# Nine products at another address distance behind each set of block products, and earlier transposes, in the first FFN of a two-layer decoder trunk

## The chip, the cores and the metric

The kernel runs on one core of a Trainium2 chip. The metric is device time in microseconds of one execution; the time before is 930.26, the median of three runs (929.63 to 930.61). TensorE multiplies (a stationary operand is loaded, a moving operand is streamed past it), VectorE and ScalarE do the element-wise work, GpSimd some of it, and the SyncE queue issues nearly all loads of weights.

## The reference, cut to what matters

Two layers over 256 tokens of width 1024. Each layer adds half an FFN, a mixer, and half an FFN again:

```python
def swiglu(x, w_gate, w_up, w_down):
    return (jax.nn.silu(x @ w_gate) * (x @ w_up)) @ w_down
...
    for layer in range(DEPTH):
        h = h + 0.5 * swiglu(rms_norm(h, ffn1_norm[layer]),
                             ffn1_w_gate[layer], ffn1_w_up[layer], ffn1_w_down[layer])
        hn = rms_norm(h, mix_norm[layer])
...
            h = h + ab_mixer(hn, ab_w_in[i], ab_v_norm[i], ab_w_spatial[i],
                             ab_b_spatial[i], ab_w_out[i])
...
        h = h + 0.5 * swiglu(rms_norm(h, ffn2_norm[layer]),
                             ffn2_w_gate[layer], ffn2_w_up[layer], ffn2_w_down[layer])
    return rms_norm(h, final_norm)
```

The FFN's inner width is 2816, which is 22 tiles of 128. All is float32. The change touches the first FFN of layer 0 and the way from it into the mixer of layer 0.

## The kernel before

**Three products for one.** A float32 product is made of three: each operand is split into a high part (ScalarE copies it to the type fp32r) and a low part (VectorE subtracts the high part). `mm3` (L384 to L387) issues high x high, high x low and low x high into one bank of PSUM. So products come in threes, with the lines L385, L386, L387.

**Weights come as chunks.** `weight_chunks` lists them in order of use; `Stream` loads each into one of three `raw` tiles, splits it into one of four pairs of tiles `whi` and `wlo`, and frees the pair when TensorE has done its chunk. The split of a chunk therefore waits until the chunk four places ahead of it is used up. A chunk of 256 columns has eight row tiles k (six in the last chunk of a down block) and gives 48 products (36).

**Two kinds of product.** In gate, up and most down products the weights are the stationary operand (128 columns of one row tile) and the activations, `xTh`/`xTl` or `hTh`/`hTl`, are streamed, 256 tokens wide. In the *block products* the roles are exchanged. The first FFN is "woven": the left 512 columns of its down product are made with seven block products (times three, 21) in place of eight for each pair of inner tiles, between the other chunks (`seven_products`, stationary `hTh`, `hTl` or their sums `hSh`, `hSl`, streamed weights). There are eleven sets of them: from the fifth gate and up pair on, one set behind each pair; the seventh follows the sixth directly, and then one behind each of the down chunks that come next. `gather_first` puts the seven results of all sets together into four quarters, which are transposed by TensorE against `ident` (`turned`, L784) and added to x.

**Address distance.** Tiles of the activations and the split tiles start on a multiple of 256 bytes in each partition. A chunk's split weights are placed `SHIFT` = 16 floats further, 64 bytes. Weights of block products are placed at 48 floats and the sums so that they start on a multiple of 256. So stationary and moving operand stand 64 bytes apart, modulo 256, in both kinds of product. A chunk with `reset` = 3 places the left 128 columns of its first three row tiles elsewhere in the tile, at 52 floats modulo 64 (208 bytes): the nine products that use them come first and have another distance. These columns and the right ones beside them are split as two strided pieces of 384 elements, the rest as one of 1280; without `reset` a chunk is split in two halves of 1024. The third chunk of this FFN and several chunks of the mixers have `reset` already.

**The way into the mixer.** `Next.pair(i, p, ...)` adds a pair of 128-row tiles of the FFN's result to x (VectorE: `part`, then `x`), makes their scaled high parts `xTh` (ScalarE) and low parts `xTl` (VectorE), and sums squares for the norm. Pairs 0 and 1 come from the transposes of the quarters, pairs 2 and 3 from the third and fourth column blocks of the down product. `first_tiles` begins the mixer: products with row tiles 0 to 5 of two column tiles, then 6 and 7, then the next chunk, where `everywhere` multiplies the split sum of squares by a matrix of ones (L478, L479); from the mean it makes `row`, which scales the queries and keys. The first scores (L1117) need a key that GpSimd finishes (L1096, L1098).

**What sets the order.** Code order, but for a scheduler that works ahead of the run: it places each engine's instructions by its own estimate of when operands are there. Each engine then works through its list in order. `issue_after` fixes some places.

Of the kernel before, what the change touches and what calls it, by code (L numbers as in the profile page):

```python
# [15 lines left out]
S = 256  # L16
# [4 lines left out]
FT = FF // 128  # L21
# [15 lines left out]
LINE, SHIFT = 64, 16  # L37
EDGE, GAP = 56, 240

RESET, RESHIFT = 3, 52  # L40
# [9 lines left out]
LAG = 4  # L50
# [5 lines left out]
def weight_chunks():  # L56

    chunks = []

    def add(m, r, n, c0, c1, shift=0, cuts=(), reset=0, summed=False, kind="N"):  # L60
        chunks.append((m[:-1], m[-1], r, n, c0, c1, shift, cuts, reset, summed, kind))

    def cols(m, c0, w, cuts=(), reset=0):
        n = CH // w
        for k in range(0, KD, n):
            add(m, k * 128, n, c0, c0 + w, SHIFT if w == 256 else 0, cuts, reset)

    def ffn(name, layer, last=False, again=(2, 3), woven=False):
        first = len(chunks)
        wd = (f"{name}_w_down", layer)  # L70

        def seven(pair):
            add(wd, pair * 256, 2, 0, 512, MSHIFT, kind="S")

        for c in range(0, FF, 256):
            if len(chunks) == 0:
                for k in (0, 4):
                    add((f"{name}_w_gate", f"{name}_w_up", layer), k * 128, 4, c, c + 256, SHIFT,
                        (1, 2, 3) if k else (0.5, 1, 1.5, 2, 3))
                continue  # L80
            for m in ("gate", "up"):
                n = len(chunks)
                cuts = (6,) if first == 0 and n in again else ()
                cols((f"{name}_w_{m}", layer), c, 256, cuts, RESET if n - first in again else 0)
            if woven and c // 256 >= LAG:
                seven(c // 256 - LAG)
        if last:
            for i in range(FT // 2):
                add(wd, i * 256, 2, 0, D, kind=LAST[i])
            return  # L90
        rest = list(range(FT // 2 - LAG, FT // 2)) if woven else []
        if woven:
            seven(rest.pop(0))
        for c in range(512 if woven else 0, D, 256):
            for k, n in DOWN:
                add(wd, k * 128, n, c, c + 256, SHIFT)
                if rest:
                    seven(rest.pop(0))

    def mix(m, order, summed=False):  # L100
        for k in order[:4:2]:
            add(m, k * 128, 2, 0, D, SHIFT)
        for c in (0, 512):
            add(m, order[4] * 128, 4, c, c + 512, SHIFT, summed=summed and c == 0)

    ffn("ffn1", 0, again=(2,), woven=0 in WOVEN)
    wab = ("ab_w_in", 0)
    cols(wab, 0, 256)
    cols(wab, 512, 256, reset=RESET)
    cols(wab, 1024, 512)  # L110
    cols(wab, 2048, 512)
    for c, n in ((1536, RESET), (1792, 0), (256, RESET), (768, RESET)):
        cols(wab, c, 256, reset=n)
    mix(("ab_w_out", 0), MIX1)
    ffn("ffn2", 0, again=(2,), woven=2 in WOVEN)
    ffn("ffn1", 1, again=(), woven=3 in WOVEN)
    wc = ("c_w_in", 0)
    for c in range(4):
        cols(wc, c * 256, 256, reset=RESET if c % 2 else 0)
        cols(wc, 1024 + c * 256, 256, reset=0 if c else RESET)  # L120
        if c % 2 == 0:
            cols(wc, 2048 + c * 256, 512)
    mix(("c_w_out", 0), MIX2, True)
    ffn("ffn2", 1, True, again=(2,))
    return chunks
# [217 lines left out]
def trunk(ctx: ExitStack, tc: tile.TileContext, a, out):  # L343
# [40 lines left out]
    def mm3(p, sh, sl, mh, ml, start, stop):  # L384
        nc.tensor.matmul(p, sh, mh, start=start, stop=False)  # L385
        nc.tensor.matmul(p, sh, ml, start=False, stop=False)  # L386
        return nc.tensor.matmul(p, sl, mh, start=False, stop=stop)  # L387
# [297 lines left out]
    def ffn(phase):  # L685
        nonlocal nxt
        with tc.tile_pool(name="fp", bufs=1) as fp:
            hT = [fp.tile([128, FT, S], F32R, name=n) for n in ("hTh", "hTl")]
            last = phase == 5
            woven = phase in WOVEN  # L690
# [99 lines left out]
            for n in range(FT):  # L790
                k, m = n - n % 2, n % 2
# [49 lines left out]
            for c in range(2 if woven else 0, 4):  # L841
                b = bank()
                for k0, n in DOWN:
                    w = st.take()
                    for kk in range(n):
                        k = k0 + kk
                        for j in range(2):
                            cs = slice(j * 128, (j + 1) * 128)
                            mm3(b[:, j * S : (j + 1) * S], w[0][kk][:, cs], w[1][kk][:, cs], hT[0][:, k], hT[1][:, k],
                                k == j == 0, k == FT - 1 and j == 1)  # L850
                    if woven and c == 3 and k0:
                        turned(k0 // 16, quarters[k0 // 16])
                    if k0 + n == FT:
                        nxt.pair(c, b, row, fp)
                    st.free()
                    if rest:
                        seven_products(rest.pop(0))
                        if not rest:
                            quarters = gather_first()
# [593 lines left out]
```

## Time and profile before

| | us |
|---|---|
| median of three runs | 930.26 |
| profiled execution | 929.4 |
| its span in the trace | 927.7 |
| TensorE busy in the span | 917.6 |
| VectorE busy | 730.0 |
| ScalarE busy | 544.9 |

The stages around the change, by their starts in TensorE's timeline: gate and up products alone to 60.80; then sets of block products between the pairs to 147.91; down products with the last sets between to 170.65; the fourth column block to 186.50, with the transposes at 181.96 and 186.50; the mixer from 186.85; its first row products (512 wide) from 200.56; the first scores at 210.01. A row of the timeline has the start, the duration, the engine, the line, the operation, what it writes and reads, and how many such instructions were merged; a matmul's duration runs to the end of its pipeline, so the pace is read from the starts. In brackets stand the idle time ahead and what ended it.

### The profile page before, as it was taken

The numbers are of one execution on the slowest core, as the hardware profiler recorded it, in microseconds if no ns is written. First come the engines' busy times: TensorE is split into PE (matmuls) and PEld (weight loads), VectorE is DVE, ScalarE is ACT, GpSimd is POOL, SyncE is SP. The second block draws the span as 40 slices with busy tenths as digits, with TensorE's granted clock in tenths as the row PEclk, the third lists the DMA queues.
The fourth block names the chain that finished last, engine by engine and source line by source line (L and its number), as shares of the span: only waits on it lengthen the run. The fifth ranks groups of instructions, "written<-read, shape, count | busy, mean of one in ns | idle before, by whom it ended". The sixth has DMA issues, their size and how long they took to land.

```text
span 927.7 us, 18344 instructions
## 1 busy us (share of the span) xinstructions
PE 917.6 (99%) x7558; PEld 898.2 (97%) x7558; DVE 730.0 (79%) x1152; ACT 544.9 (59%) x830; POOL 84.0 (9%) x117
## 2 busy tenths in 40 slices
PE   9999999999999999999999999999999999999997
PEld 9999999988999999999999999999999999999886
DVE  7999797888878856675677766757788799978896
ACT  7766455568667644444564444445776767545574
POOL 0000000016220000000000000001555200000002
PEclk9999999999999999999999999999999999999999
DMA  9646555754336587785656877855533466755691
GB/s 322 248 160 228 192 179 189 258 204 164 131 127 242 223 272 273 273 295 177 221 184 246 302 270 297 344 201 210 182 137 137 108 231 229 274 195 204 221 311 58
DMA packets 34707, 202.17 MB, mean 218 GB/s; under 512 B 3984, under 2 KB 6288, under 8 KB 13760
## 3 DMA queue, kind: packets, MB, share of 16 engines
q1 hardware_dynamic: 33120, 197.79, 59.6%
q0 software_dynamic: 496, 1.77, 0.8%
q10 hardware_dynamic: 1008, 1.44, 0.4%
q8 instruction: 59, 0.97, 0.4%
q14 instruction: 24, 0.20, 0.1%
HBM read 188.14 MB, written 12.85 MB: 217 GB/s over the span
## 4 chain that ended last, share of the span: by engine, by line
PE 91%; issue 4%; DVE 2%; DMA 1%; POOL 1%; ACT 1%; POOLq 0%; DVEq 0%
PE bank L386 29%; PE bank L385 29%; PE bank L387 29%; DVE wlo L253 1%; PE bank L633 1%; PE bank L1155 1%; DMA x<-blocks 1%; DMA xTl<-away 0%; PE bank L636 0%; PE bank L609 0%; POOL xTl L899 0%; ACT whi L246 0%; PE bank L1117 0%; PE bank L1119 0%; PE bank L1118 0%
## 5 line engine op out<-in xcount | busy, mean ns | idle before, releaser
L246 ACT ACTIVATE whi<-raw 128x1024 fp32r<-128x1024 f32 (+5 forms) x359 | 340.8, 991 | 243.1 <-PE bank L386 110.2
L253 DVE TENSOR_TENSOR wlo<-raw,whi 128x1024 fp32r<-128x1024 f32 (+5 forms) x359 | 402.2, 1148 | 56.5 <-ACT whi L246 55.3
L385 PE MATMUL bank<-xTh,whi 128*128 128x256 f32 x1600 | 443.3, 277 | 1.3 <-ACT xTh L421 1.3
L386 PE MATMUL bank<-xTl,whi 128*128 128x256 f32 x1600 | 442.4, 277 | 0.4 <-DVE xTl L424 0.4
L387 PE MATMUL bank<-xTh,wlo 128*128 128x256 f32 x1600 | 442.3, 277 | 0.0
L385 PEld LDWEIGHTS bank<-xTh,whi 128*128 128x128 f32 x1600 | 300.3, 188 | 1.6 <-ACT xTh L421 1.5
L386 PEld LDWEIGHTS bank<-xTl,whi 128*128 128x128 f32 x1600 | 300.9, 188 | 0.6 <-DVE xTl L424 0.6
L387 PEld LDWEIGHTS bank<-xTh,wlo 128*128 128x128 f32 x1600 | 300.2, 188 | 0.0
L385 PE MATMUL bank<-hTh,whi 128*128 128x256 f32 x440 | 121.9, 277 | 0.0
L387 PE MATMUL bank<-hTh,wlo 128*128 128x256 f32 x440 | 121.8, 277 | 0.0
L386 PE MATMUL bank<-hTl,whi 128*128 128x256 f32 x440 | 121.8, 277 | 0.0
L386 PEld LDWEIGHTS bank<-hTl,whi 128*128 128x128 f32 x440 | 82.9, 188 | 0.0
L385 PEld LDWEIGHTS bank<-hTh,whi 128*128 128x128 f32 x440 | 82.6, 188 | 0.0
L387 PEld LDWEIGHTS bank<-hTh,wlo 128*128 128x128 f32 x440 | 82.6, 188 | 0.0
L720 DVE TENSOR_TENSOR hm<-gs,bank 128x512 f32<-128x512 f32 x44 | 29.9, 684 | 33.4 <-PE bank L387 33.2
L1050 POOL MEMSET k<- 64x256 f32 x12 | 3.2, 306 | 572.0 <-ACT whi L246 379.2
L717 DVE TENSOR_TENSOR gs<-bank,row 128x512 f32<-128x512 f32 x44 | 30.1, 685 | 11.4 <-PE bank L387 11.3
L1146 POOL TENSOR_SCALAR pr<-pr,rl 128x128 f32<-128x128 f32 (+1 forms) x36 | 34.0, 957 | 25.8 <-DVE rl L1142 18.6
L718 ACT ACTIVATE gs<-gs 128x512 f32<-128x512 f32 x44 | 27.2, 621 | 14.7 <-DVE gs L717 14.7
L385 PE MATMUL bank<-mixh,whi 128*128 128x256 f32 x128 | 35.7, 279 | 0.0
L387 PE MATMUL bank<-mixh,wlo 128*128 128x256 f32 x128 | 35.4, 277 | 0.0
L386 PE MATMUL bank<-mixl,whi 128*128 128x256 f32 x128 | 35.4, 276 | 0.0
(247 smaller groups left out, 1152.4 us busy)
## 6 DMA issues: line engine op xcount, KB each, us to landing
raw<-in_weights SPq DMA_DIRECT2D x135, 1024.0 KB, 5.0
blocks<-in_weights SPq DMA_DIRECT2D x9, 1024.0 KB, 11.1
blocks<-blocks SPq DMA_DIRECT2D x9, 1024.0 KB, 8.7
raw<-in_weights SPq DMA_DIRECT2D x17, 512.0 KB, 3.6
raw<-in_weights SPq DMA_DIRECT2D x10, 768.0 KB, 6.3
raw<-blocks SPq DMA_DIRECT2D x7, 1024.0 KB, 4.7
raw<-in_weights SPq DMA_DIRECT2D x7, 256.0 KB, 4.6
blocks<-block SPq DMA_DIRECT2D x5, 256.0 KB, 8.8
```

The source lines that it names most:

```text
L246: done = nc.scalar.activation(hi, r, AF.Copy)
L253: self.made[u] = done, nc.vector.tensor_sub(lo, r, hi.bitcast(F32))
L385: nc.tensor.matmul(p, sh, mh, start=start, stop=False)
L386: nc.tensor.matmul(p, sh, ml, start=False, stop=False)
L387: return nc.tensor.matmul(p, sl, mh, start=False, stop=stop)
L633: nc.tensor.matmul(o, w[0][i][:, cs], xT[m][:, k], start=k == 0 and m == "h" and j % 2 == 0, stop=False)
L717: nc.vector.tensor_mul(g, both(pg), twice(norm["row"]))
L718: nc.scalar.activation(g, g, AF.Silu)
L720: nc.vector.tensor_mul(hm, g, both(pu))
L1050: nc.gpsimd.memset(pair[j][o, 1].bitcast(F32), 0.0)
L1146: share = engine.tensor_scalar(pr[:, cs], pr[:, cs], rl[:, b : b + 1], None, op0=ALU.mult)
L1155: nc.tensor.transpose(tp[:, i * 128 : (i + 1) * 128], pr[:, i * 128 : (i + 1) * 128], ident)
```

## The change

Three things change. (1) The gate chunks of the sixth to the eleventh gate and up pair, all behind a set of block products, get `reset` = 3. (2) So do the four down chunks that stand behind a set of block products; for this the down loop takes the left columns of the first three row tiles first, then their right columns, then the rest as before. This order holds for the down chunks of the second and third FFN too, which have no `reset`. (3) The two sets of transposes, which stood behind the second and the third chunk of the fourth column block, now stand within the second: behind its fourth and its seventh row tile.

```diff
@@ weight_chunks
-                cols((f"{name}_w_{m}", layer), c, 256, cuts, RESET if n - first in again else 0)
+                cols((f"{name}_w_{m}", layer), c, 256, cuts,
+                     RESET if n - first in again or woven and m == "gate" and c // 256 > LAG else 0)
...
+        behind = woven
...
-                add(wd, k * 128, n, c, c + 256, SHIFT)
+                add(wd, k * 128, n, c, c + 256, SHIFT, reset=RESET if behind else 0)
+                behind = bool(rest)
@@ ffn
-                    for kk in range(n):
+                    turns = [(j, kk) for kk in range(RESET, n) for j in range(2)]
+                    for j, kk in [(j, kk) for j in range(2) for kk in range(RESET)] + turns:
                         k = k0 + kk
-                        for j in range(2):
-                            cs = slice(j * 128, (j + 1) * 128)
-                            mm3(b[:, j * S : (j + 1) * S], w[0][kk][:, cs], w[1][kk][:, cs], hT[0][:, k], hT[1][:, k],
-                                k == j == 0, k == FT - 1 and j == 1)
-                    if woven and c == 3 and k0:
-                        turned(k0 // 16, quarters[k0 // 16])
+                        cs = slice(j * 128, (j + 1) * 128)
+                        mm3(b[:, j * S : (j + 1) * S], w[0][kk][:, cs], w[1][kk][:, cs], hT[0][:, k], hT[1][:, k],
+                            k == j == 0, k == FT - 1 and j == 1)
+                        if woven and c == 3 and k0 == 8 and j and kk in (3, 6):
+                            turned(kk // 6, quarters[kk // 6])
                     if k0 + n == FT:
                         nxt.pair(c, b, row, fp)
```

In the new file every line of `Stream` and behind stands three further down. How instructions move is shown at three places. The first is TensorE in the second chunk of the fourth column block. `bank_2291` takes the transposes of the first pair, `hm_2198` is the first quarter, `whi_2106` and `wlo_2107` are the chunk's weights. Now:

```order
L389 MATMUL bank_2208<-hTl_96,whi_2106 128x256
L390 MATMUL bank_2208<-hTh_95,wlo_2107 128x256
L787 MATMUL bank_2291<-ident_84,hm_2198 128x128 x4
L388 MATMUL bank_2208<-hTh_95,whi_2106 128x256
L389 MATMUL bank_2208<-hTl_96,whi_2106 128x256
```

Before, these four transposes stood behind the last product of this chunk, 24 products later, and the other four behind the 36 products of the third chunk; now the others stand 18 products behind the first four.

The second place is VectorE around the three last pairs, from the first pair's `part` on (`wlo_2311` and `wlo_2382` are weights of the mixer). Before:

```order
L434 TENSOR_TENSOR part_2300<-bank_2295,half_470 128x512
L253 TENSOR_TENSOR wlo_2311<-raw_2145,whi_2310 128x1024
L435 TENSOR_TENSOR x_90<-part_2300,x_90 128x512
L253 TENSOR_TENSOR wlo_2311<-raw_2145,whi_2310 128x1024
L424 SCALAR_TENSOR_TENSOR xTl_1887<-x_90,gT_82,xTh_1886 128x256 x2
L452 TENSOR_TENSOR acc_2137<-acc_2137,sq_2307 128x512
L434 TENSOR_TENSOR part_2359<-bank_2354,half_470 128x512
L253 TENSOR_TENSOR wlo_2382<-raw_2174,whi_2381 128x1024
L435 TENSOR_TENSOR x_90<-part_2359,x_90 128x512
L253 TENSOR_TENSOR wlo_2382<-raw_2174,whi_2381 128x1024
L424 SCALAR_TENSOR_TENSOR xTl_1887<-x_90,gT_82,xTh_1886 128x256 x2
```

Now (the same two chunks are `wlo_2347` and `wlo_2402`; `part_2390` is the last pair):

```order
L437 TENSOR_TENSOR part_2329<-bank_2324,half_470 128x512
L455 TENSOR_TENSOR acc_2157<-acc_2157,sq_2303 128x512
L438 TENSOR_TENSOR x_90<-part_2329,x_90 128x512
L256 TENSOR_TENSOR wlo_2347<-raw_2165,whi_2346 128x1024
L427 SCALAR_TENSOR_TENSOR xTl_1903<-x_90,gT_82,xTh_1902 128x256 x2
L256 TENSOR_TENSOR wlo_2347<-raw_2165,whi_2346 128x1024
L455 TENSOR_TENSOR acc_2157<-acc_2157,sq_2336 128x512
L437 TENSOR_TENSOR part_2390<-bank_2208,half_470 128x512
L458 TENSOR_TENSOR acc_2157<-acc_2157 128x256
L438 TENSOR_TENSOR x_90<-part_2390,x_90 128x512
L256 TENSOR_TENSOR wlo_2402<-raw_2194,whi_2401 128x1024
L427 SCALAR_TENSOR_TENSOR xTl_1903<-x_90,gT_82,xTh_1902 128x256 x2
```

The first pair's `part`, `x` and `xTl` now stand directly ahead of these rows with no split among them; one split half stands ahead of the second pair's `xTl`, and one ahead of the last pair's. Behind the last row one more half stands between the two last sums of squares.

The third place is ScalarE in the same stretch, from the first pair's high parts on. Before, a split (`whi_2310`) stood ahead of these rows:

```order
L421 ACTIVATE xTh_1886<-x_90,gT_82 128x256 x2
L448 ACTIVATE sq_2307<-x_90 128x512
L246 ACTIVATE whi_2381<-raw_2174 128x1024 x2
L421 ACTIVATE xTh_1886<-x_90,gT_82 128x256 x2
L448 ACTIVATE sq_2366<-x_90 128x512
```

Now:

```order
L424 ACTIVATE xTh_1902<-x_90,gT_82 128x256 x2
L451 ACTIVATE sq_2303<-x_90 128x512
L249 ACTIVATE whi_2346<-raw_2165 128x1024 x2
L424 ACTIVATE xTh_1902<-x_90,gT_82 128x256 x2
L451 ACTIVATE sq_2336<-x_90 128x512
L249 ACTIVATE whi_2401<-raw_2194 128x1024 x2
```

The split of the first of the two chunks moved behind the first pair, and that of the second behind the second pair; the last pair's high parts follow. On TensorE the products of the mixer's beginning, which before alternated between three column tiles, now stand tile by tile (18, 18, 12, 12), and the first product with ones stands behind 60 of them, where it stood behind 72.

## The prediction

> **What bounds the kernel now.** I read the page first, then TensorE's timeline stage by stage, then the waits around the end of the first FFN.
>
> ```profile
> span 927.7 us, 18344 instructions
> ...
> PE 917.6 (99%) x7558; PEld 898.2 (97%) x7558; DVE 730.0 (79%) x1152; ACT 544.9 (59%) x830; POOL 84.0 (9%) x117
> ...
> PE 91%; issue 4%; DVE 2%; DMA 1%; POOL 1%; ACT 1%; POOLq 0%; DVEq 0%
> ```
>
> TensorE is busy for 99% of the span and is 91% of the chain that ended last. So time can come from two things only: products that start further apart than they must, and the few waits. The starts in the timeline give the first:
>
> ```profile
> 28.16 0.28 PE L385 MATMUL bank<-xTh,whi 128*128 128x256 f32 x1
> ...
> 60.80 0.28 PE L385 MATMUL bank<-whi,hTh 128*128 128x256 f32 x1
> ...
> 63.28 0.28 PE L385 MATMUL bank<-xTh,whi 128*128 128x256 f32 x1
> ...
> 74.59 0.29 PE L385 MATMUL bank<-whi,hTh 128*128 128x256 f32 x1
> ...
> 76.99 0.28 PE L385 MATMUL bank<-xTh,whi 128*128 128x256 f32 x1
> ...
> 88.30 0.29 PE L385 MATMUL bank<-whi,hTh 128*128 128x256 f32 x1
> ...
> 170.65 0.28 PE L385 MATMUL bank<-hTh,whi 128*128 128x256 f32 x1
> ...
> 181.96 0.60 PE L784 MATMUL bank<-ident,hm 128*128 128x128 f32 x4
> ```
>
> From 28.16 to 60.80 stand 288 gate and up products: 32.64 / 288 = 113.3 ns from start to start, the fast pace. Behind the first set of block products (21 products, 60.80 to 63.28) the same kind of product goes slower: 96 of them from 63.28 to 74.59, 11.31 us, 117.8 ns. It is 11.31 again from 76.99 to 88.30, and again for the 96 down products from 170.65 to 181.96. No wait stands in these stretches; the granted clock is full (1.00 in the window quoted further down). Once taken, a pace lasts until something ends it.
>
> The block products have the two paces too. The first set, entered from the fast pace, takes 2.48 us (118 ns each); the second, entered from the slow pace at 74.59, takes 2.40 (114). The waits are in one place:
>
> ```profile
> PE bank L385 <- ACT xTh L421: 1.3, 1, 1.3
> PE bank L1117 <- POOL k L1098: 1.1, 1, 1.1
> PE bank L386 <- DVE xTl L424: 0.4, 1, 0.4
> ```
>
> TensorE waits at the start of the mixer for the second pair of the new x (the pair behind the second set of transposes), and then for the first key.
>
> **The nine products.** What ends the 118 ns pace is shown in the second mixer, in a chunk which already begins at the other distance:
>
> ```profile
> 662.66 0.63 PE L1126 MATMUL bank<-k,q 128*128 128x256 f32 x4
> 663.13 0.28 PE L385 MATMUL bank<-xTh,whi 128*128 128x256 f32 x1
> ...
> 664.19 0.28 PE L385 MATMUL bank<-xTh,whi 128*128 128x256 f32 x1
> ...
> 665.89 0.28 PE L1117 MATMUL bank<-k,q 128*128 128x256 f32 x1
> ```
>
> The four score products ahead go at 118 ns (0.47 / 4), the slow pace, behind products that have the weights as moving operand, as block products have. Then nine products take 1.06 us (117 ns), and the other 15 take 1.70 (113.3). So I price a chunk with the new start at 1.06 us for nine products and 113.3 ns for each that follows, and let the up chunk behind a gate chunk keep the pace, as 28.16 to 60.80 keeps it through chunk borders.
>
> Gate and up, six times: 1.06 + 87 x 0.1133 = 10.92 in place of 11.31, 0.39 each, **2.35 us**. Down, third column block: 48, 48 and 36 products, each behind a set of block products, at 117.8 now; 1.06 plus 39, 39 and 27 products at 113.3 gain 0.17, 0.17 and 0.12, **0.47**. The fourth column block (96 products, 0.39) is counted with the transition. Bounds: nothing, if these nine do not end that pace behind block products; 0.04 a chunk more, if they ran fast themselves.
>
> Against it stands the first set of block products: entered from the fast pace it was slow. After the change all ten later sets are entered from there (the sixth and seventh follow each other). At 2.48 in place of 2.40 that is 0.08 for each of eight, and for the pair 42 x 0.0045 less what its first products lose already, 0.16: **minus 0.80 us**. Bounds: nothing to 0.80. I take the upper, since the one set entered from the fast pace is the only row of that kind.
>
> The weight splits of a changed chunk become three pieces. The groups of VectorE's splits from 60 to 180 us by size (count, busy us, mean ns):
>
> ```profile
> L253 DVE TENSOR_TENSOR wlo<-raw,whi 128x1024 fp32r<-128x1024 f32 x41 | 49.1, 1219 | 3.2 <-ACT whi L246 3.2
> L253 DVE TENSOR_TENSOR wlo<-raw,whi 128x1280 fp32r<-128x1280 f32 x1 | 1.5, 1493 | 0.4 <-ACT whi L246 0.4
> L253 DVE TENSOR_TENSOR wlo<-raw,whi 128x384 fp32r<-128x384 f32 x2 | 1.0, 553 | 0.0
> ```
>
> and one period of the loop in the table of windows (busy us of PE, PEld, DVE, ACT, POOL, then the clock):
>
> ```profile
> 88.30:102.00 13.70, 13.70 (x119) 13.70 (x118) 11.32 (x16) 7.49 (x9) 0.00 (x0) 1.00 0.59 197
> ```
>
> Two of 1219 ns become 1493 + 2 x 553: 0.16 us more on VectorE per changed chunk. A period (gate, up, block products) has 13.70 us, of which VectorE works 11.32; the new one has about 13.4 and 11.5. It stays covered: 0. Without cover it would be 10 x 0.16 = 1.6 us.
>
> **The transition.** VectorE and ScalarE run in the order that is written, so I carry the old durations through the new order. Rows of before, by engine:
>
> ```profile
> 186.50 0.60 PE L784 MATMUL bank<-ident,hm 128*128 128x128 f32 x4
> 186.85 0.37 PE L385 MATMUL bank<-xTh,whi 128*128 128x256 f32 x1
> ...
> 200.56 0.40 PE L385 MATMUL bank<-whi,xTh 128*128 128x512 f32 x1
> ...
> 208.52 0.39 PE L387 MATMUL bank<-whi,xTl 128*128 128x512 f32 x1
> 210.01 0.38 PE L1117 MATMUL bank<-k,q 128*128 128x256 f32 x1 [1.10 <-POOL k L1098]
> ```
>
> ```profile
> 178.57 1.49 DVE L253 TENSOR_TENSOR wlo<-raw,whi 128x1280 fp32r<-128x1280 f32 x1 [0.44 <-ACT whi L246]
> 182.59 0.69 DVE L434 TENSOR_TENSOR part<-bank,half 128x512 f32<-128x512 f32 x1 [2.53 <-PE bank L784]
> ...
> 187.47 0.68 DVE L434 TENSOR_TENSOR part<-bank,half 128x512 f32<-128x512 f32 x1
> ...
> 190.94 0.88 DVE L424 SCALAR_TENSOR_TENSOR xTl<-x,gT,xTh 128x256 fp32r<-128x256 f32 x2
> ...
> 193.26 0.69 DVE L435 TENSOR_TENSOR x<-part,x 128x512 f32<-128x512 f32 x1
> 194.53 0.89 DVE L424 SCALAR_TENSOR_TENSOR xTl<-x,gT,xTh 128x256 fp32r<-128x256 f32 x2 [0.58 <-ACT xTh L421]
> ...
> 197.39 0.43 DVE L390 TENSOR_TENSOR mixl<-acc,mixh 128x256 fp32r<-128x256 f32 x1 [1.05 <-ACT mixh L390]
> 198.36 0.42 DVE L480 TENSOR_SCALAR qk<-bank 128x256 f32<-128x256 f32 x1 [0.54 <-PE bank L479]
> ```
>
> ```profile
> 185.05 0.91 ACT L421 ACTIVATE xTh<-x,gT 128x256 fp32r<-128x256 f32 x2 [0.95 <-DVE x L435]
> 185.87 0.62 ACT L448 ACTIVATE sq<-x 128x512 f32<-128x512 f32 x1
> 186.62 2.02 ACT L246 ACTIVATE whi<-raw 128x1024 fp32r<-128x1024 f32 x2
> ```
>
> ```profile
> 209.23 0.72 POOL L1098 TENSOR_TENSOR k<-qk,k 64x256 fp32r<-64x256 f32 x1
> ```
>
> Count from 170.65, the fourth column block's start. *Before:* first product of the mixer at 16.20 (186.85), second pair's low parts from 20.29, first score at 39.36.
>
> *TensorE after:* first chunk 1.06 + 39 x 0.1133 = 5.48; 24 products to 8.20; four transposes 0.35; 18 products (0.10 late behind transposes) to 10.69; transposes; the last six to 11.82; the 36 of the third chunk to 15.90. There the mixer begins.
>
> *First pair:* VectorE comes to it at about 9.2 (its last piece of a split ended at 180.06, 3.8 after the first chunk's end at 176.30 before, and that end is now 5.48). Product with the row and sum into x at steps of 0.6 to 0.7, high parts on ScalarE 10.6 to 11.5, low parts 11.1 to 12.0. *Second pair:* 11.9 (its transposes end at 11.0); x by 13.8. Its high parts stand on ScalarE behind a weight split of 2.02 that waits for the second chunk's buffer: 12.0 to 14.0, high parts to 14.9, low parts to 15.8. The mixer's first product on them is its seventh, at 16.6: it finds them. *Last pair:* behind one split half and a sum, VectorE takes it at 17.4; x by 19.0; another half (1.22) stands ahead of the low parts, 20.1 to 21.0. TensorE wants the first at 15.90 + 36 x 0.1133 = 20.0, waits 0.65, and 0.1 for the next. *Mean:* sums, a split half of 1.22 between them, ScalarE, low part by 23.8; TensorE comes to its two products with ones after 60 and 63 others, 23.3 and 23.8: about 0.1. The other 33 products end at 27.7.
>
> From there 36 wide products take 208.52 + 0.23 - 200.56 = 8.2: TensorE is at the first score at 35.9. The key: mean at 24.2; from 198.36 to the end of the key's low part (209.23 + 0.72) lie 11.6 with the same VectorE work, so 35.8. Both ways give 35.9 in place of 39.36: 3.45 less; I take **3.2**, since each of some ten hand-overs that I round may be 0.03 late. Bounds: all that TensorE loses there, 13.71 less 98 products (11.2) and 210.01 less 208.75, is 2.5 + 1.3; with the chunks' 0.39 that makes 4.2. Below, minus 1 (the last rival).
>
> In the later FFNs only the order of the first 18 of each chunk's products changes; all stay at one distance: 0.
>
> **The sum:** 2.35 + 0.47 - 0.80 + 3.2 = 5.2. The profiled execution took 929.4 us, 1.7 around its span; it would take 924.2. The median of the runs is 930.26, which becomes 925.0: **925.0 us** is the forecast.
>
> **Rivals.** *The block products keep their pace* (15%): the slow first set has only one witness, and later sets use other buffers. Then 0.8 comes back: 924.2.
>
> *The distance is no cause* (12%): the nine products do not end that pace behind block products, which is not the situation of 663.13 in each detail, and only the transposes gain. 3.2 - 0.39 = 2.8: 927.4. [...]
>
> *The wait moves* (15%): two split halves (2.4 us) come between the new x and the row on VectorE, or the last pair waits longer. Half the transition is lost: 5.2 - 1.7 = 3.5, 926.8. For it: VectorE and ScalarE have splits among these steps in the new order; against: their buffers come free in time by my count.
>
> *No change* (6%): neither pace nor waits gain more than the block products lose: 930.
>
> *Slower* (5%): TensorE meets the products with ones after 60 products, not 72 as before, and 33 others queue behind them. The low part was ready at 197.82 before, 27.2 by this count, 23.8 in mine. If the moved work leaves it there, TensorE stands 3.4 us, and each us beyond is lost whole. It decides from about 29.3 on: the 2.1 of the chunks are eaten then. At 31 the time is 932.
>
> **How the numbers follow.** The forecast has 47%. A measurement of this kernel tells 0.2% (1.9 us) from no change. Faster by more: 47 + 15 + 12 + 15 = 89%; within, 6%; slower, 5%. The range, 923.9 to 927.6, takes in three of the rivals and leaves the last two and the tails out.
>
> **What would show it.** Gate and up pairs behind the block products at 10.9 us, of which the first nine products at 117 ns; sets of block products at 2.48 (right) or 2.40 (second way). No wait for the second pair at the mixer's start, 0.6 to 0.8 for the last one, none or little at the first score, which stands 36 us behind the fourth column block's start. The forecast is wrong if gate pairs stay at 11.3, or if a wait over 1 us stands in the mixer's first 20 us.

## The result

The changed kernel takes 923.37 us (median of four timings, 922.95 to 924.23), against 929.94 for the kernel before beside it (929.49 to 930.61). The ratio is 0.993, with a 95% interval of 0.9913 to 0.9947. That is 6.6 us faster, where 5.2 were forecast, and 0.5 below the range of 923.9 to 927.6. The profiled execution took 923.03 us. Two of the later timings of the kernel before, of 1018.49 and 3854.38 us, are in a slow state and are left out of all that follows.

### The profile page after: what moved, and what is told of

It reads as the page before. It is cut to its first block, busy times and chain, and to the rows that moved or that the text cites. A ratio compares the mean times of both kernels' runs of the same rounds, so it can differ in the third digit from the quotient of the medians.

```text
span 921.3 us, 18362 instructions
## 1 busy us (share of the span) xinstructions
PE 913.7 (99%) x7558; PEld 894.8 (97%) x7558; DVE 730.4 (79%) x1162; ACT 545.0 (59%) x840; POOL 82.1 (9%) x117
## 4 chain that ended last, share of the span: by engine, by line
PE 92%; issue 4%; DVE 2%; DMA 1%; ACT 0%; POOL 0%; POOLq 0%; DVEq 0%
PE bank L388 29%; PE bank L389 29%; PE bank L390 29%; DVE wlo L256 1%; PE bank L636 1%; PE bank L1158 1%; DMA x<-blocks 1%; DMA xTl<-away 0%; PE bank L612 0%; PE bank L639 0%; POOL xTl L902 0%; ACT whi L249 0%; PE bank L1120 0%; PE bank L1122 0%; DVE xTl L427 0%
## 5 line engine op out<-in xcount | busy, mean ns | idle before, releaser
L393 ACT ACTIVATE hTh<-hm 128x512 fp32r<-128x512 f32 x44 | 27.1, 619 | 12.8 <-DVE hm L723 11.9
```

The costliest lines, as they stand in the source:

```text
L393: return nc.scalar.activation(hi, src, AF.Copy), nc.vector.tensor_sub(lo, src, hi.bitcast(F32))
```

## The profile after

The page of the changed kernel, its span, its engines and its chain of waits:

```profile
span 921.3 us, 18362 instructions
...
PE 913.7 (99%) x7558; PEld 894.8 (97%) x7558; DVE 730.4 (79%) x1162; ACT 545.0 (59%) x840; POOL 82.1 (9%) x117
...
PE 92%; issue 4%; DVE 2%; DMA 1%; ACT 0%; POOL 0%; POOLq 0%; DVEq 0%
```

TensorE has the same 7558 products and is 3.9 us less busy; the span is 6.4 shorter. What bounds the kernel has not changed. TensorE's timeline at the borders of the stages:

```profile
62.54 0.28 PE L388 MATMUL bank<-xTh,whi 128*128 128x256 f32 x1
...
63.59 0.28 PE L388 MATMUL bank<-xTh,whi 128*128 128x256 f32 x1
...
73.45 0.28 PE L388 MATMUL bank<-whi,hTh 128*128 128x256 f32 x1
...
75.92 0.28 PE L388 MATMUL bank<-xTh,whi 128*128 128x256 f32 x1
...
86.84 0.28 PE L388 MATMUL bank<-whi,hTh 128*128 128x256 f32 x1
...
167.81 0.28 PE L388 MATMUL bank<-hTh,whi 128*128 128x256 f32 x1
...
183.72 0.28 PE L388 MATMUL bank<-xTh,whi 128*128 128x256 f32 x1
...
195.57 0.40 PE L388 MATMUL bank<-whi,xTh 128*128 128x512 f32 x1
...
203.75 0.37 PE L1120 MATMUL bank<-k,q 128*128 128x256 f32 x1
```

Nine products go from 62.54 to 63.59 (117 ns each), the other 87 of the pair to 73.45 (113.3). The pair takes 10.91 us where it took 11.31, and 10.92 again from 75.92 to 86.84. The set of block products between them, 73.45 to 75.92, takes 2.48 where it took 2.40.

From the fourth column block (167.81) to the first score (203.75) are 35.94 us, where it was 39.36. The score's row has no bracket: TensorE does not wait for the key any more. In the stretch from 165 to 206 us the waits hold one row, and the windows show where TensorE still stands idle (span, then busy us of PE, PEld, DVE, ACT, POOL, the clock, DMA):

```profile
PE bank L389 <- DVE xTl L427: 0.4, 1, 0.4
```

```profile
183.72:195.57 11.85, 11.50 (x101) 11.30 (x99) 10.84 (x16) 7.47 (x10) 3.37 (x9) 1.00 0.72 258
195.57:203.75 8.18, 8.18 (x38) 6.59 (x37) 7.85 (x18) 4.63 (x9) 1.13 (x3) 1.00 0.76 248
87.00:100.39 13.39, 13.39 (x120) 13.39 (x119) 11.39 (x17) 7.59 (x11) 0.00 (x0) 1.00 0.62 202
```

The mixer's products up to the row products take 11.85 us (13.71 before) with 0.35 idle. The last row is a whole period of the loop: TensorE is busy for all of it, so the extra pieces of the weight splits are hidden, 11.39 of VectorE in 13.39.

Stage by stage, from the starts in the two timelines (us):

| stage | before | after | difference | forecast |
|---|---|---|---|---|
| to the first set of block products | 60.80 | 60.06 | -0.74 | 0 |
| first set to fourth column block | 109.85 | 107.75 | -2.10 | -2.02 |
| fourth column block to first score | 39.36 | 35.94 | -3.42 | -3.2 |
| first score to last product | 710.91 | 710.89 | -0.02 | 0 |

The two stages that the change touches gain 5.52. The 0.74 ahead of them is no effect of the change: the products there are the same, and in the thirteen traces of this study the first set of block products starts anywhere from 59.89 to 60.80, with two traces of the kernel before itself at the two ends. Between the 5.52 of the two stages and the 6.6 between the medians about 1 us was left to explain.

## The experiments

In all experiments the stages are read from TensorE's starts, as above. A first group, beside 21 timings of the kernel before (median 929.35, 928.55 to 930.75):

| kernel | median, us | ratio, 95% interval | first set to fourth block | fourth block to score |
|---|---|---|---|---|
| gate chunks only | 928.17 | 0.9986 (0.9977 to 0.9994) | 108.02 | 40.50 |
| down chunks only | 929.47 | 0.9998 (0.9989 to 1.0006) | 109.58 | 39.05 |
| transposes only | 925.91 | 0.9957 (0.9945 to 0.997) | 109.85 | 36.11 |
| all, but usual distance | 925.90 | 0.9957 (0.9944 to 0.9971) | 109.85 | 36.19 |

**The gate chunks alone.** The kernel before, with the nine products of the six gate chunks.

```diff
-                cols((f"{name}_w_{m}", layer), c, 256, cuts, RESET if n - first in again else 0)
+                cols((f"{name}_w_{m}", layer), c, 256, cuts,
+                     RESET if n - first in again or woven and m == "gate" and c // 256 > LAG else 0)
```

> Part 1 alone: the six gate chunks behind block products begin with nine products at the other distance; down chunks and transposes as before. Theory (distance sets the pace, a pace lasts until something ends it): gate and up pairs behind block products 10.91 us in place of 11.31, 6 x 0.395 = 2.4 less; the first seven sets of block products 2.48 us, those entered from a fast pair 0.075 longer than before and the pair of sets 4.95 in place of 4.79, so 0.5 more; down chunks unchanged at 117.8 ns, the last three sets at 2.40. From the first set of block products to the fourth column block 107.9 us in place of 109.85; in all 1.85 less than before, about 928.1. Rival (distance is no cause): pairs stay at 11.31, 0 within 0.3. A second question, for all runs of this call: the first 28 us hold no changed instruction, yet they differed by 0.74 us between the two profiled executions. Theory: they vary from run to run for every kernel; rival: the changed kernel begins sooner each time.

The six pairs took 10.91, the first six sets 2.48, the two sets that follow each other 4.95, the last three sets, entered from the slow pace, 2.40: the stage is 1.83 shorter. (The two that follow each other are the seventh and the eighth of the eleven, behind the last gate and up pair, and not the sixth and seventh as said ahead of the result and in the prediction; the count of ten later sets is right.) But the stage behind it was 1.14 *longer* than in the kernel before, though its work is the same. The time, too, is only 1.2 less than that of the kernel before, where 1.85 were expected. This stretch is taken up below.

**The down chunks alone.** The kernel before, with the nine products and the new order in the down loop.

```diff
+        behind = woven
...
-                add(wd, k * 128, n, c, c + 256, SHIFT)
+                add(wd, k * 128, n, c, c + 256, SHIFT, reset=RESET if behind else 0)
+                behind = bool(rest)
...
-                    for kk in range(n):
+                    turns = [(j, kk) for kk in range(RESET, n) for j in range(2)]
+                    for j, kk in [(j, kk) for j in range(2) for kk in range(RESET)] + turns:
```

> Part 2 alone: the four down chunks behind block products begin with nine products at the other distance, in the changed order of products; gate chunks and transposes as before. Theory: the three down chunks of the third column block 5.48, 5.48 and 4.12 us in place of 5.65, 5.65 and 4.24; the fourth column block's first two chunks 10.92 in place of 11.31; the three sets of block products that follow a fast down chunk 2.48 in place of 2.40. From the first set to the fourth column block 109.6 in place of 109.85, and from there to the first score 39.0 in place of 39.36: 0.6 less in all, about 929.3. Rival: 0. The order of the second and third FFN's down chunks, changed here too, does nothing: 113.3 ns there.

The three chunks took 5.47, 5.47 and 4.11 (5.65, 5.65 and 4.24 before), the three sets that they reach 2.48: 0.27 gained there and 0.31 behind the fourth block's start. The times cannot tell 0.6 us from nothing; the trace can.

**The transposes alone.** The kernel before, with both sets of transposes within the second chunk.

```diff
-                    if woven and c == 3 and k0:
-                        turned(k0 // 16, quarters[k0 // 16])
+                        if woven and c == 3 and k0 == 8 and kk in (3, 6):
+                            turned(kk // 6, quarters[kk // 6])
```

> Part 3 alone: the two sets of transposes stand behind the fourth and the seventh row tile of the fourth column block's second chunk; no new distance anywhere. Theory: from the first set of block products to the fourth column block 109.85 as before; from there to the first score 36.3 in place of 39.36 (35.94 with all parts; 0.39 of that is the new distance's, less 0.1 since the first transposes end the slow pace by themselves, as they did before). TensorE's wait for the second pair (1.3 + 0.4) is gone, the wait at the first score 0.3 at most. 3.1 less in all, about 926.8. Rival (the moved work only moves the wait): 1.7 less or nothing.

The stage to the first score is 3.25 shorter (36.11, where 36.3 was expected), the time 3.4 (3.1 was expected). The stage gains of the three parts, 1.83, 0.58 and 3.25, add up to 5.66 (the gate chunks' in their own stage only), against 5.52 for all together.

**Everything but the distance.** The changed kernel, in which the nine products' weights stand at the usual 16 floats. Order, pieces of the splits and transposes are as in the change; `kind` is "D" for the ten chunks alone.

```diff
-        far = nk * w - reset * h + RESHIFT // LINE * LINE + RESHIFT
+        far = nk * w - reset * h + (SHIFT if kind == "D" else RESHIFT // LINE * LINE + RESHIFT)
```

> The changed kernel, but the nine products' weights of the ten chunks are placed at the usual distance, 16 floats past the line in place of 52: same order of products, same three pieces of the split, same transposes, only the address differs. Theory: the pace is not ended: pairs at 11.31, sets of block products back at 2.40, down chunks at 117.8 ns, and only the transposes gain: 109.85 us from the first set to the fourth column block, then about 36.3 to the first score, in all as part 3 alone, about 926.8. Rival (the order of products, or the pieces, end the pace): as the changed kernel, pairs at 10.91, about 923.4.

The first changed pair of chunks in its timeline, from its first product to the next set:

```profile
62.94 0.28 PE L389 MATMUL bank<-xTh,whi 128*128 128x256 f32 x1
...
74.25 0.29 PE L389 MATMUL bank<-whi,hTh 128*128 128x256 f32 x1
```

It takes 11.31 us, as before the change, the sets take 2.40, the down chunks 5.65, and the time is that of the transposes alone (925.90 and 925.91). So the address of the nine products' weights is the cause of the pace; neither the new order nor the pieces do anything for it. Only weights were moved, and no run moved the activations: that it is the distance between the two operands, and not the place of the weights alone, is not shown. What is shown are two kernels that differ in a placement alone and stand 0.40 us apart in a pair of chunks and 2.1 in the stage.

**How many products, and the block products too.** Beside these stands the changed kernel once more, to see what in its result repeats.

> The changed kernel itself, once more. Its trace gave 10.91 us for a gate and up pair, 2.48 for a set of block products, 35.94 from the fourth column block to the first score. Theory: these three come again to within 0.05, because they follow from addresses and from order; only the first 16 us (same code in both kernels, where products start at half pace until the clock is granted) differ from run to run, by up to 0.8. Time 923.4, within 0.6, and a mean granted clock of 0.998 or 0.999 in all runs, since no wait of about 1 us is left at the mixer's beginning. Rival (the 0.5 us beyond my range came from one lucky comparison): the median is 924.5 or above.

It took 923.19 (922.61 to 923.63, ratio 0.993, 0.9917 to 0.9944), beside 929.47 for the kernel before; its stages were 107.75 and 35.93, its first set of block products started at 60.49. The stages repeat to 0.01 and the start does not. (The half pace that the expectation puts there shows in the first profile of the kernel before: its first twelve products of 256 columns took 2.64 us, 4.50 to 7.14, 220 ns each, and the next eight 0.92, 115 each. After the change only the first four were slow, 198 ns each from 4.33 to 5.12, and the next four took 115. The record of the granted clock in these two traces begins at 7.01 and 4.83.) Inside the last stage one pace did not repeat either. Two rows of this second trace, behind the second set of transposes:

```profile
179.56 0.28 PE L389 MATMUL bank<-hTl,whi 128*128 128x256 f32 x1
...
184.39 0.28 PE L388 MATMUL bank<-xTh,whi 128*128 128x256 f32 x1
```

These 41 products took 4.83 us (118 ns each). In the first trace of this kernel the same 41, from 179.07 to 183.72, took 4.65 (113). So addresses and order do not settle the pace everywhere; what else does is open. It cost nothing here: the wait for the last pair's low parts, 0.35 us in the first trace, was gone, and the product that had waited there started 20.62 us after the fourth column block's start in both.

One kernel used three products in place of nine at the other distance in the ten chunks:

```diff
-                     RESET if n - first in again or woven and m == "gate" and c // 256 > LAG else 0)
+                     RESET if n - first in again else 1 if woven and m == "gate" and c // 256 > LAG else 0)
...
-                add(wd, k * 128, n, c, c + 256, SHIFT, reset=RESET if behind else 0)
+                add(wd, k * 128, n, c, c + 256, SHIFT, reset=1 if behind else 0)
```

> After, with three products in place of nine at the other distance in the ten changed chunks (the later chunks with nine keep them). Theory A (it is enough that the row of products at the usual distance is broken once): the pairs stay at 10.9, and six products fewer at 117 ns gain 10 x 0.02 = 0.2 us; about 923.2. Theory B (the pace is ended only by a stretch of some length): the pairs go back to 11.3 and the sets to 2.40, as where the nine had the usual distance: 925.9. My trace of the unchanged chunks only shows nine, so it tells nothing for three; I lean to A at 55 to 45.

Three are enough: the pairs take 10.90, the stage 107.63 (0.12 less than with nine; 0.2 was expected), the time is 923.28, which cannot be told from 923.19.

Another placed the weights of the first nine block products of every set at the other distance:

```diff
+            at7 = [(MRESET if i < 3 else shift) + i * q for i in range(7)]
+            self.parts[u] = tuple([t[:, i : i + q] for i in at7] for t in (his, los))
...
-            split(shift, raw[:, q : 4 * q])
+            split(MRESET, raw[:, q : 4 * q])
```

Here `MRESET` is 12 floats.

> After, with the weights of the first nine products of every set of block products placed at 12 floats in place of 48, so that these nine too have another distance (208 bytes modulo 256). Theory (one rule for both kinds of product: any set entered from the fast pace goes slow unless its first products have another distance): sets go from 2.48 to 2.41 (nine at 117 ns, twelve at 113.3), the pair from 4.95 to 4.81; eleven sets, -0.8 us against after, about 922.6. Rival (block products are slow behind fast products for another reason, for instance the moving weights themselves): sets stay at 2.48, time stays at after's; or worse, the chunk behind them loses its fast pace, 11.3 a pair, +2.

A set in its timeline, at the first product, the tenth, the sixteenth, and the one behind the set:

```profile
73.31 0.28 PE L390 MATMUL bank<-whi,hTh 128*128 128x256 f32 x1
...
74.37 0.28 PE L390 MATMUL bank<-whi,hTh 128*128 128x256 f32 x1
...
75.08 0.28 PE L390 MATMUL bank<-whi,hSh 128*128 128x256 f32 x1
...
75.76 0.28 PE L390 MATMUL bank<-xTh,whi 128*128 128x256 f32 x1
```

Nine products take 1.06, but the next six, which have the usual distance, take 0.71 (118 ns), and only the last six 0.68 (113). A set takes 2.45 rather than 2.41: the rule holds in direction for block products, at less than half of the size. Why six more are slow there is open. The stage is 107.45, 0.30 less than after the change; the time, 923.03, is not measurably less.

Both together, to see whether they add:

> The changed kernel with the nine products of the block products at the other distance too, and one product group of three in place of nine in the ten chunks. Each alone gave 107.46 and 107.63 from the first set of block products to the fourth column block, where the changed kernel has 107.75. Theory (they add): 107.3 to 107.4, 0.4 us less than the changed kernel, about 922.8. Rival: three products do not end the pace that fifteen products of the set have left; pairs above 10.95.

The pairs took 10.89, the sets 2.45, the stage 107.28: they add (0.30 + 0.12 is 0.42, measured 0.47). The time is 923.18 (ratio 0.9933, 0.9921 to 0.9946). No variant beats the changed kernel by more than a measurement can tell.

**The stretch that got longer.** In the gate kernel's profile the mixer's first products, up to the row products, took 15.12 us; in the kernel before, 13.71, with the same work and the same waits of 1.3 and 0.4. Its windows have the granted clock in the last column but two:

```profile
187.60:188.80 1.20, 0.62 (x4) 0.42 (x4) 1.20 (x3) 1.07 (x3) 0.00 (x0) 1.00 0.07 27
188.80:192.20 3.40, 3.40 (x16) 3.40 (x17) 2.83 (x6) 0.89 (x3) 0.78 (x4) 0.50 0.78 270
```

Behind the waits the clock was at half for 3.40 us, and a product took 213 ns. Nothing in the edit touches that place, so the kernel before was profiled a second time.

> The kernel before, one more look, for the mixer's beginning. In the trace of before the products behind the waits of 1.3 and 0.4 us kept 113 ns; in the kernel with the gate chunks' part alone they ran at 213 ns for some 3 us behind the same waits, which cost 1.2 to 1.4. Of 21 timings of before five had a mean granted clock of 0.996 or 0.997 and took 930.0 to 930.8, the others 928.6 to 930.1. Theory (the waits let the clock fall back in some executions): either this look has 0.996 and a half-pace stretch between the mixer's start and its row products (15.1 in place of 13.7 us), or it has 0.998 and none. Rival (the stretch can lie anywhere): a look at 0.996 with 13.7 there.

The second execution (929.89 us) had it. Its windows, and its timeline behind the wait:

```profile
185.94:191.70 5.76, 4.06 (x33) 3.66 (x32) 5.76 (x10) 3.22 (x5) 0.00 (x0) 1.00 0.61 196
191.70:195.10 3.40, 3.40 (x18) 3.40 (x17) 2.75 (x7) 1.43 (x3) 1.86 (x8) 0.50 0.89 342
195.10:201.20 6.10, 6.10 (x55) 6.10 (x53) 2.95 (x5) 4.13 (x5) 0.91 (x3) 1.00 0.38 133
```

```profile
189.57 0.62 PE L385 MATMUL bank<-xTh,whi 128*128 128x256 f32 x3 [1.33 <-ACT xTh L421]
190.56 0.39 PE L386 MATMUL bank<-xTl,whi 128*128 128x256 f32 x1 [0.37 <-DVE xTl L424]
...
191.74 0.42 PE L385 MATMUL bank<-xTh,whi 128*128 128x256 f32 x1
191.96 0.42 PE L386 MATMUL bank<-xTl,whi 128*128 128x256 f32 x1
192.18 0.41 PE L387 MATMUL bank<-xTh,wlo 128*128 128x256 f32 x1
```

TensorE waited 1.33 and 0.37 us, ran at full pace again, and then, from 191.74, at half pace for 3.40 us. The row products started 15.26 us after the mixer, and the first score, counted from the fourth column block, came 1.28 later than in the first profile of this same kernel. Both stretches, 188.80 to 192.20 with the gate chunks alone and 191.70 to 195.10 here, are 3.40 us long; what sets that length is not shown.

To see whether the waits are the cause, one kernel made them longer and one shorter. Longer: the kernel before, with both sets of transposes behind the third chunk.

```diff
-                    if woven and c == 3 and k0:
-                        turned(k0 // 16, quarters[k0 // 16])
+                    if woven and c == 3 and k0 == 16:
+                        turned(0, quarters[0])
+                        turned(1, quarters[1])
```

> The kernel before, with both sets of transposes behind the third chunk of the fourth column block (the first set comes 36 products later than before). Work is the same; the waits at the mixer's beginning become longer. Theory (a wait of about 1.5 us or more there lets TensorE's clock fall to half in a part of the executions: a mean clock of 0.996 or 0.997 was seen in 22 of 52 timings of kernels with that wait and in none of 29 without it): the waits grow to 3 to 5 us in all, the fourth column block's start to the first score takes 41 to 43 us in place of 39.4, and at least half of the timings show 0.997 or below. Rival (the lower clock has to do with something else in these kernels, such as the chunks' pace): the share of such timings stays at about one in three, or the clock stays at 0.998 and only the waits are added.

It took 931.87 us (ratio 1.0026, 1.0015 to 1.0037), and the stage to the first score 42.27. Its waits and one window:

```profile
PE bank L385 <- ACT xTh L421: 2.9, 2, 2.6
PE bank L1118 <- POOL k L1099: 0.8, 1, 0.8
PE bank L386 <- DVE xTl L424: 0.4, 1, 0.4
```

```profile
191.50:194.90 3.40, 3.16 (x16) 2.87 (x15) 3.33 (x7) 1.43 (x3) 0.00 (x0) 0.50 0.64 267
```

Half the clock for 3.40 us once more. Shorter: the changed kernel, with the second set of transposes back behind the third chunk.

```diff
-                        if woven and c == 3 and k0 == 8 and j and kk in (3, 6):
-                            turned(kk // 6, quarters[kk // 6])
+                        if woven and c == 3 and k0 == 8 and j and kk == 3:
+                            turned(0, quarters[0])
+                    if woven and c == 3 and k0 == 16:
+                        turned(1, quarters[1])
```

> The changed kernel with the second set of transposes back behind the third chunk, the first set early. Theory: the first set is worth little by itself, because the second pair is the one that TensorE waits for: the second pair's sum ends at 17.7, its high parts at 18.6 and low parts at 19.5, counted from the fourth column block's start, where TensorE wants them at 18.3; waits of 0.4 to 0.6 and again 0.4 to 0.7, and the last pair a little later, the first score at 36.5 to 38 in place of 35.94; time 924.2 to 925.5. With waits this short the clock stays at 0.998 or above in all timings. Rival (the first set is what freed VectorE, the second could have stayed): the score at 36.0 to 36.4 and the time of the changed kernel to within 0.4.

It took 926.82 us (ratio 0.9973, 0.9963 to 0.9984). The stage to the first score took 39.06, not 36.5 to 38. The 0.3 that it is shorter than in the kernel before is the gain of the nine products: with the down chunks alone, and both sets late, it took 39.05. So the first set alone gains nothing, and the second one, or the two together, carries the gain. Its waits in the mixer, and VectorE around the second pair:

```profile
PE bank L1122 <- POOL k L1103: 1.1, 1, 1.1
PE bank L388 <- ACT xTh L424: 0.9, 1, 0.9
PE bank L389 <- DVE xTl L427: 0.4, 1, 0.4
```

```profile
184.71 0.69 DVE L437 TENSOR_TENSOR part<-bank,half 128x512 f32<-128x512 f32 x1 [0.97 <-PE bank L787]
185.32 1.22 DVE L256 TENSOR_TENSOR wlo<-raw,whi 128x1024 fp32r<-128x1024 f32 x1
186.45 0.68 DVE L438 TENSOR_TENSOR x<-part,x 128x512 f32<-128x512 f32 x1
187.06 1.22 DVE L256 TENSOR_TENSOR wlo<-raw,whi 128x1024 fp32r<-128x1024 f32 x1
188.19 0.87 DVE L427 SCALAR_TENSOR_TENSOR xTl<-x,gT,xTh 128x256 fp32r<-128x256 f32 x2
```

I had expected the pair without splits in between. Two halves of 1.22 stand among its steps, as in the kernel before, and the mean, the row and the key come later by as much; the key is waited for 1.1 again. The waits at the beginning, 0.9 and 0.4, are only 0.4 shorter in all.

The mean granted clock of each timing is a sign of how often the half pace came: 0.997 or below in 6 of 7 with the longer waits, 12 of 43 of the kernel before (the timings beside these experiments), 7 of 11 with the gate chunks alone, 6 of 11 with the down chunks alone; in none of 42 of the kernels whose waits at the mixer's start are 0.9 and 0.4 or less (the changed kernel, the five variants with both sets early, and the one with the first set early). The profiles say the same: three of the five with waits of 1.3 us or more hold such a stretch (the gate chunks alone, the second of the kernel before, the longer waits). Of the eight others four took 35.93 to 36.19 us from the fourth column block to the first score, where a stretch had added 1.14 and 1.28 us to 39.36, and two more have a mean of 0.999. The kernel before took 930.18 in the median where the mean was lower and 929.15 elsewhere.

The mean is a rough sign only. The first profiles of the kernel before and of the changed kernel also have half the clock at their very end, when TensorE has done its last product: before, the window from 925 to 926 us has 0.60 and what follows 0.50, which makes 2.5 us to the span's end; after, 919 to 920 has 0.80 and what follows 0.50, 1.7 us. The last products start at 920.92 and 914.65. An estimate from these lengths: a stretch of 3.40 us lowers the mean over 928 us by 0.0018, such an end by 0.0009 to 0.0013. The profiled execution with the longer waits took 931.76 us and has a mean of 0.998, with the stretch of 191.50 in it. So the counts can miss some.

So the half pace goes with the length of these waits, and in the kernel before it costs about 1 us (an estimate from 930.18 and 929.15). Two things are open: why the chunk variants, with the same waits, meet it more often than the kernel before, and what it costs with the longer waits, since no timing of that kernel is known to be without it.

## Why the prediction was right or wrong

**The nine products: right.** Pairs at 10.91 (10.92 forecast), the down chunks 5.47, 5.47 and 4.12, which is 0.18, 0.18 and 0.12 less (0.17, 0.17 and 0.12). The rival that distance is no cause fell with the run that kept all but the new placement.

**The block products: right.** All ten later sets took 2.48, or 4.95 for the pair, as the one witness had it. The rival by which they keep their pace fell in the same trace.

**The splits at nothing: right.** 11.39 of VectorE in a period of 13.39.

**The transition: right step by step, then shaded.** The prediction's ledger is its list of steps, counted from the fourth column block. The rows that it spoke of, VectorE first, then ScalarE, then GpSimd:

```profile
176.97 0.68 DVE L437 TENSOR_TENSOR part<-bank,half 128x512 f32<-128x512 f32 x1
...
179.76 0.68 DVE L437 TENSOR_TENSOR part<-bank,half 128x512 f32<-128x512 f32 x1
...
182.69 0.88 DVE L427 SCALAR_TENSOR_TENSOR xTl<-x,gT,xTh 128x256 fp32r<-128x256 f32 x2
...
185.22 0.68 DVE L437 TENSOR_TENSOR part<-bank,half 128x512 f32<-128x512 f32 x1
...
187.90 0.88 DVE L427 SCALAR_TENSOR_TENSOR xTl<-x,gT,xTh 128x256 fp32r<-128x256 f32 x2
...
191.06 0.42 DVE L393 TENSOR_TENSOR mixl<-acc,mixh 128x256 fp32r<-128x256 f32 x1 [0.48 <-ACT mixh L393]
```

```profile
181.70 0.90 ACT L424 ACTIVATE xTh<-x,gT 128x256 fp32r<-128x256 f32 x2
```

```profile
202.95 0.74 POOL L1101 TENSOR_TENSOR k<-qk,k 64x256 fp32r<-64x256 f32 x1
```

Counted from 167.81: the first pair's `part` at 9.16 (9.2 forecast), the second's at 11.95 (11.9), its high parts at 13.89 (14.0), its low parts done at 15.76 (15.8), the last pair's `part` at 17.41 (17.4), its low parts 20.09 to 20.97 (20.1 to 21.0), the mean's low part done at 23.67 (23.8), the row products at 27.76 (27.7), the first score at 35.94 (35.9). The key is done at 203.69, 0.06 ahead of the score, so both ways arrive together, as they did in the ledger. One sign came out otherwise: the wait for the last pair shows as 0.35 us, not 0.6 to 0.8. The profile counts a wait from the end of the product ahead, and the 0.28 us of a product are longer than the 0.11 between two starts; by the starts, the 60 products took 7.50 us where 113.3 ns each make 6.80, and that 0.70 is near the 0.65 and 0.1 of the ledger. The ledger gave 3.45, and 3.42 came. What was taken was 3.2, for late hand-overs that no row showed; that lost 0.2. The rivals of the moved wait and of the late mean fell: no wait over 0.4 stands there.

**What failed is the base of the sum,** "The median of the runs is 930.26, which becomes 925.0", **and a gain that the sum put at nothing.** The median that was used, of three timings, lay high: the 43 timings of the kernel before have a median of 929.33, and from there 5.2 leads to 924.1. From the profiled execution the prediction's own sum came to 924.2. The nine timings of the changed kernel together have a median of 923.19, so of the 1.8 us by which the forecast was too high, 0.9 is the base and 0.9 the gain (5.2 forecast, 6.14 between the two medians).

Of this second 0.9, 0.3 is in the two stages: 5.52 against 5.2, most of it the shading. Another part is a term that the sum does not have: with the waits gone, the half pace behind them goes too. By the mean clock that is some 3 in 10 executions, for about 1 us each, so about 0.3 on average (an estimate from 12 of 43 and 930.18 less 929.15). The remaining 0.3 I cannot place. The timings of the kernel before without a lowered mean clock (929.15) still stand 5.96 above the changed kernel, not 5.52. Since the mean can miss a stretch, some may hide in them; whether that is enough is not settled.

The range has the same fault at its lower end: 923.9 leaves room for one term at its bound (with 4.2 for the transition the sum gives 924.1) and none for the base, which moved 0.9 between three timings and 43. With the base at 929.33 the range would have held the result.

## What to carry to other kernels

A ledger that carries measured durations through the new order of each engine was right to some 0.1 us in a stretch of 36; then its result should be taken as it stands and not shaded. The base needs its own uncertainty: set the sum against the median of many timings, or give the range what few timings leave open. Where TensorE waits as long as here, 1.33 and 0.37 us in the midst of dense work, look at the granted clock in windows of some 3 us behind the wait, in more than one profile: the half clock lasted 3.40 us in three of the five profiles with waits of 1.3 us or more, and removing such a wait can gain more than the wait (about 1 us here, by the estimate from 930.18 and 929.15).

## What the runs showed of the hardware

A 256-wide product of this kernel has two paces at the full granted clock (1.00 in the windows), 113.3 and 118 ns. Which one it takes hangs on where the weights are placed (10.91 us for a pair of chunks with the nine products placed elsewhere, 11.31 with them at the usual distance) and on what ran before (a set of block products took 2.40 us behind a slow pair and 2.48 behind a fast one), and behind a set of transposes the same kernel showed 113 ns for 41 products in its first trace and 118 in its second. For weights as stationary operand, three products with their weights placed elsewhere end the slow pace (10.90 for the pair); for weights as moving operand nine did not end it at once: they took 1.06 us, the next six still 118 ns each, and the last six 113.

Two waits of 1.33 and 0.37 us can be followed by 3.40 us at half the granted clock, with 213 ns for a product: two of the four profiles with these waits have it, and so has the one with waits of 2.6 and 0.4. The pause between the second wait's end and the drop differs: 0 with the gate chunks alone (both at 188.80), 1.1 us in the second profile of the kernel before (190.56 to 191.70).
